# Flat matmul operands, two tiles for the recurrence's values, and the memory's operand made in another stage of a two-layer decoder trunk

## The chip, the cores and the metric

One NeuronCore of one Trainium2 chip runs the whole program. The metric is the device time of one execution in microseconds (us); smaller is better. TensorE (PE) multiplies matrices out of SBUF into PSUM, VectorE (DVE) and ScalarE (ACT) do elementwise work and read PSUM, GpSimd (POOL) does a little elementwise work, and SyncE (SP) issues the DMA transfers. Each engine works through its own instructions in order, and the engines wait for one another by semaphores.

## The reference, cut to what matters

Sequence 256, width 1024, two layers. Each layer runs five sub-layers on the residual stream x:

```python
x = x + 0.5 * swiglu(rms_norm(x, ffn1_norm[l]), ffn1_w_gu[l], ffn1_w_down[l])
z = rms_norm(x, mix_norm[l]) @ w_in[l]
y_a = dilated_attention(q_a, k_a, v_a) @ w_att_branch[l]
o_b = rms_norm(hgrn2_recurrence(q_b, f_b, i_b, lb_all[l]), head_norm) * silu(og_b)
y_b = o_b @ w_hgrn_branch[l]
x = x + (sigmoid(gate_a) * y_a + sigmoid(gate_b) * y_b) @ w_mix_out[l]
x = x + cross_attention(rms_norm(x, xattn_norm[l]), rms_norm(mem, mem_norm[l]), wq, wkv, wo)
x = x + 0.5 * swiglu(rms_norm(x, ffn2_norm[l]), ffn2_w_gu[l], ffn2_w_down[l])
```

The result is a last rms_norm of x. All is float32; the memory `mem` (256 tokens) is an input and the same for both layers.

## The kernel before

The weights are streamed once. A chunk of 16 weight blocks of 128x128 (1 MB) is loaded by SP into `raws`; for each half of a chunk (8 blocks) ACT casts a high part (`whi`, L104) and DVE subtracts it to get a low part (`wlo`, L110). Operands are split in the same way: an `Act` holds for each block of 128 features 256 columns of high and 256 columns of low part side by side, two blocks to a buffer of the pool `big` (23 buffers, named `slot`).

A feature-major product (`fm`, L308 to L323) takes one or two columns of weight blocks. For each block PE runs the high part against the operand's 512 columns (L320) and the low part against its 256 high columns (L321); both add up in PSUM. PSUM is the pool `psum` with four tiles of 1024 columns (`pair`); `bank()` takes a whole such tile and uses half of it. When a product is done, ACT copies one half out (L327), and DVE adds the other at the next tick (L330).

The order of the work beside the products is set by ticks. `Stream.take` calls `tick` once for each half chunk, so once for 8 weight blocks. Each engine's instructions are then in program order (`manual_schedule`). A tick runs deferred work that is due, and then one step of `urgent`, or else one step of a generator in `sides`. While something is urgent, finished products wait with their evacuation.

Four of these pieces bear on the change:

- **The norms.** A sub-layer's operand is x times a gain; the factor of the rms norm is found beside the first products. `Norm.steps` sums squares on PE (L368), takes DVE's mean (L371), POOL's power (L374) and DVE's diagonal (L377), and one tick later PE broadcasts it (L382) and ACT copies it (L384). Eight sub-layers have one, and the memory's statistics have one more (`keep`).
- **The recurrence.** `hgrn` runs twice a layer. At L648 and L650 PE makes the values of the two halves of the sequence, i = 0 and i = 1, in the two halves of one `pair`; ACT squares each half (L652). The tile is read once more by DVE at L661 at a later step.
- **The branches.** After all products from `w_in`, `mixer` multiplies the two branches into the merged operand `mg` (12 blocks for each of 8 columns j) and then multiplies by `w_mix_out`. For each j ACT runs L327 and L275, DVE L330, L866, L868 and L278.
- **The memory's operand.** `mem_operand` loads `mem` (two transfers of 512 KB) and, four steps later, makes the high and low parts of 8 blocks in four steps of two (L285 on ACT, L286 on DVE). It is put in `sides` as the branches begin, so it runs beside them; `xattn` uses it.

```python
both_tiles = pair()
bs = [both_tiles[:, :512], both_tiles[:, 512:]]
```

Of the kernel before, what the change touches and what calls it, by code (L numbers as in the profile page):

```python
# [16 lines left out]
T = 256  # L17
# [110 lines left out]
def build(tc, a, nchunks):  # L128
    nc = tc.nc
    ctx = ExitStack()  # L130
    ent = ctx.enter_context
# [1 line left out]
    raws = ent(tc.tile_pool(name="raws", bufs=3))  # L133
    his = ent(tc.tile_pool(name="his", bufs=5))
    los = ent(tc.tile_pool(name="los", bufs=4))
    big = ent(tc.tile_pool(name="big", bufs=23))
    mid = ent(tc.tile_pool(name="mid", bufs=4))
    tmps = ent(tc.tile_pool(name="tmps", bufs=10))
    tiny = ent(tc.tile_pool(name="tiny", bufs=2))
# [7 lines left out]
    def tmp():  # L147
        return tmps.tile([P, T], F32, name="tmp")

    def pair():  # L150
        return psum.tile([P, 1024], F32, name="pair")

    def bank():
        return pair()[:, :512]

    def join():
        return joins.tile([P, 2 * T], F32, name="join")

    def two(t):
        return t.rearrange("p (i t) -> p i t", i=2)  # L160

    def both(t):
        return t[:, None].to_broadcast([P, 2, T])

    deferred, sides, flags = [], [], set()
# [4 lines left out]
    def defer(n, fn):  # L170
        deferred.append([n, fn])
# [127 lines left out]
    def after(evac):  # L299
        pending.append(evac)  # L300
        if not urgent:
            flush()
# [5 lines left out]
    def fm(items, evac):  # L308

        b = pair().rearrange("p (i h t) -> p i h t", i=2, h=2)
        ks = [item[4] for item in items]
        order = [(k, i) for k in range(max(ks)) for i in range(len(items)) if k < ks[i]]
        if len(set(ks)) > 1:
            order.sort(key=lambda o: o[1])
        for k, i in order:
            name, l, c, act, K = items[i]
            wh, wl = W.take([(name, l, k * P, c)])
            nc.tensor.matmul(b[:, i], wh, two(act.parts(k)), start=k == 0, stop=False)  # L320
            nc.tensor.matmul(b[:, i, 0], wl, act.hi(k), start=False, stop=k == K - 1)  # L321
        n = len(items)
        after(lambda: evac(b[:, :n, 0], b[:, :n, 1]))  # L323

    def add_halves(d, left, right, then, now=False):

        nc.scalar.copy(d, right)  # L327

        def add():
            nc.vector.tensor_tensor(d, left, d, op=OP.add)  # L330
            then()
        if now:
            add()
        else:
            defer(1, add)
# [13 lines left out]
    class Norm:  # L349
# [15 lines left out]
        def steps(self, keep=None):  # L365
            st = bank()
            for i in range(2):
                nc.tensor.matmul(st[:, i:i + 1], self.acc[:, i * P:(i + 1) * P], ones[:, :1],  # L368
                                 start=True, stop=True)
            ms = tiny.tile([P, 2], F32, name="ms")  # L370
            nc.vector.tensor_scalar(ms, st[:, :2], 1.0 / D, EPS, op0=OP.mult, op1=OP.add)  # L371
            pool = tiny if keep is None else consts
            self.r = pool.tile([P, 2], F32, name="rstd" + (keep or ""))
            nc.gpsimd.tensor_tensor(self.r, ms, mhalf[:, :2], op=OP.pow)  # L374
            dg = tmp()
            for i in range(2):
                nc.vector.tensor_scalar(dg[:, i * P:(i + 1) * P], ident, self.r[:, i:i + 1], None, op0=OP.mult)  # L377
            yield
            if keep:
                yield  # L380
            b = bank()
            nc.tensor.matmul(b[:, :T], ones, dg, start=True, stop=True)  # L382
            self.bc = (tiny if keep is None else consts).tile([P, T], F32, name="bc" + (keep or ""))
            nc.scalar.copy(self.bc, b[:, :T])  # L384

    def urgent_norm(n, more=None):
        def run():
            for _ in range(n.wait):
                yield
            yield from n.steps()  # L390
            if more:
                more()
        urgent.append(run())
# [67 lines left out]
    def mm_resid(name, l, act, K, res):  # L461
        n = 2 if K == KD else 1
        for j in range(0, KD, n):
            fm([(name, l, (j + i) * P, act, K) for i in range(n)],
               lambda left, right, j=j: res.take(j, left, right))


    def ffn(pre, l, res, nxt):
        h, n = res.act, res.norm
        urgent_norm(n)  # L470
        act = Act()
        for j in range(KF):
            def evac(left, right, j=j):
                last = j == KF - 1
                t, s = join(), tmp()
                u = t[:, T:]

                def stage1():
                    nc.vector.tensor_tensor(two(t), two(t), both(n.bc), op=OP.mult)  # L479
                    nc.scalar.activation(s, t[:, :T], AF.Silu)  # L480
                    if last:
                        stage2()
                    else:
                        defer(1, stage2)

                def stage2():
                    nc.vector.tensor_tensor(u, s, u, op=OP.mult)
                    act.put(j, u, later=0 if last else 1)
                add_halves(two(t), left, right, stage1, last)
            fm([(pre + "_w_gu", l, c, h, KD) for c in (j * P, FF + j * P)], evac)  # L490
        r = nxt()
        mm_resid(pre + "_w_down", l, act, KF, r)
        return r
# [74 lines left out]
    def mem_operand(l, hm):  # L568
        m = load_mem()
        yield from [None] * 4  # L570
        for j in range(KD):
            hm.put_gain(j, m(j), vec("mem_norm", l, j))
            if j % 2 == 1:
                yield


    def hgrn(l, hh, Q, K, F, ib, sog, out):
# [4 lines left out]
        b = bank()  # L582
# [11 lines left out]
        for li, B in enumerate((1, 2, 4, 8, 16, 32, 64)):  # L594
            W2 = max(2 * B, 32)
            h = W2 // 2
            b = bank()
# [23 lines left out]
            else:  # L621
                for g in range(P // W2):
                    r = slice(W2 * g, W2 * g + B)
                    nc.scalar.copy(lohi(AT)[r, :, W2 * g + B:W2 * g + W2],
                                   b[r, :8 * B].rearrange("p (c u) -> p c u", u=B))
            if B == 16:
                for g in range(4):
                    r = slice(32 * g, 32 * g + 32)
# [3 lines left out]
        b = bank()  # L632
        for h in range(4):
            nc.tensor.matmul(b[:, h * P:(h + 1) * P], lohi(K)[:, 2 * h], lohi(QP)[:, 2 * h + 1],
                             start=True, stop=True)
# [2 lines left out]
        while ("i", l) not in flags:  # L638
            yield True
        ss = tiny.tile([P, 8], F32, name="ss")  # L640
        both_tiles = pair()
        bs = [both_tiles[:, :512], both_tiles[:, 512:]]
        for i in range(2):
            b = bs[i]
            for h in range(4):
# [20 lines left out]
        for i in range(2):  # L666
            b = bank()
# [4 lines left out]
            for h in range(2):  # L672
                k = 4 * hh + 2 * i + h
# [61 lines left out]
    def mixer(l, res, nxt):  # L735
        h, n = res.act, res.norm
# [118 lines left out]
            gate(j)  # L855
        drain()
        mg = Act()
        hm = Act()
        sides.append(mem_operand(l, hm))
        for j in range(KD):  # L860
            def evac(left, right, j=j):
                last = j == KD - 1
# [8 lines left out]
            fm([("w_att_branch", l, j * P, aout, AH), ("w_hgrn_branch", l, j * P, hout, HH)], evac)  # L871
        r = nxt()
        mm_resid("w_mix_out", l, mg, KD, r)
        return r, hm


    def scores(h, q, k):
# [79 lines left out]
    def resid(name, l, scale):  # L957
        return lambda: Resid(lambda j: vec(name, l, j), scale)

    r = resid("ffn1_norm", 0, 0.5)()  # L960
# [18 lines left out]
        yield from lower_bounds()  # L979
    sides.append(setup())  # L980
    for l in range(L):
        r = ffn("ffn1", l, r, resid("mix_norm", l, 0.5))
        r, hm = mixer(l, r, resid("xattn_norm", l, 1.0))
        r = xattn(l, r, hm, resid("ffn2_norm", l, 1.0))
        r = ffn("ffn2", l, r, resid("ffn1_norm", l + 1, 0.5) if l + 1 < L else Last)
    ctx.close()
# [62 lines left out]
```

## Time and profile before

| what | value |
|---|---|
| median of 3 runs | 1673.91 us (1673.47 to 1674.52) |
| the profiled execution's own time | 1671.91 us |
| its span | 1670.1 us |
| PE busy | 1638.0 us, 98% |
| PE weight loads busy | 1417.4 us, 85% |
| DVE busy | 1243.2 us, 74% |
| ACT busy | 924.5 us, 55% |
| mean granted clock of TensorE | 0.995 |

The span is the time from the first to the last instruction of the program; the execution's own time has 1.8 us more around it. Matmuls are pipelined and their ends are modelled, so a busy PE says little: what counts is from one matmul's start to the next one's. A wait is listed as the idle time of an engine before an instruction, with the instruction that ended it.

### The profile page before, as it was taken

The numbers are of one execution on the slowest core, as the hardware profiler recorded it, in microseconds if no ns is written. First come the engines' busy times: TensorE is split into PE (matmuls) and PEld (weight loads), VectorE is DVE, ScalarE is ACT, GpSimd is POOL, SyncE is SP. The second block draws the span as 40 slices with busy tenths as digits, with TensorE's granted clock in tenths as the row PEclk, the third lists the DMA queues.
The fourth block names the chain that finished last, engine by engine and source line by source line (L and its number), as shares of the span: only waits on it lengthen the run. The fifth ranks groups of instructions, "written<-read, shape, count | busy, mean of one in ns | idle before, by whom it ended". The sixth has DMA issues, their size and how long they took to land.

```text
span 1670.1 us, 26491 instructions
## 1 busy us (share of the span) xinstructions
PE 1638.0 (98%) x10818; PEld 1417.4 (85%) x10818; DVE 1243.2 (74%) x1813; ACT 924.5 (55%) x1389; POOL 77.3 (5%) x61
## 2 busy tenths in 40 slices
PE   8999999999998999999999999999999989999998
PEld 7888888888887888888888888888888878888887
DVE  8886696767868868776677767867687688687764
ACT  6665445556665555555456544446565656565542
POOL 2000000111100000000000000010110000000000
PEclk9999999999999999999999999999999999999999
DMA  7555544443444544555455555444444445354552
GB/s 285 186 184 192 185 163 167 152 177 137 166 168 153 184 152 165 189 179 200 177 180 198 184 194 178 168 145 167 152 152 156 172 168 186 126 200 179 184 190 80
DMA packets 41738, 288.94 MB, mean 173 GB/s; under 512 B 4881, under 2 KB 5009, under 8 KB 7441
## 3 DMA queue, kind: packets, MB, share of 16 engines
q1 hardware_dynamic: 41328, 286.73, 47.5%
q8 instruction: 85, 1.39, 0.3%
q10 hardware_dynamic: 288, 0.52, 0.1%
q14 instruction: 37, 0.29, 0.1%
HBM read 286.18 MB, written 1.05 MB: 172 GB/s over the span
## 4 chain that ended last, share of the span: by engine, by line
PE 77%; DVE 11%; issue 8%; ACT 2%; POOL 1%; DMA 1%; SPq 0%; POOLq 0%; ACTq 0%; DVEq 0%
PE pair L320 41%; PE pair L321 21%; DVE wlo L110 4%; PE pair L295 3%; PE pair L297 3%; PE pair L296 3%; PE pair L603 1%; DVE join L330 1%; DVE slot L286 1%; DVE join L866 1%; PE pair L688 1%; PE pair L722 1%; DVE x L407 1%; DMA raw<-w 1%; PE pair L648 0%
## 5 line engine op out<-in xcount | busy, mean ns | idle before, releaser
L320 PE MATMUL pair<-slot,whi 128*128 128x512 f32 x3840 | 1362.0, 399 | 8.2 <-DVE slot L278 7.2
L321 PE MATMUL pair<-slot,wlo 128*128 128x256 f32 x3840 | 1077.0, 280 | 5.6 <-DVE wlo L110 3.9
L320 PEld LDWEIGHTS pair<-slot,whi 128*128 128x128 f32 x3840 | 724.1, 189 | 179.1 <-ACT whi L104 7.8
L321 PEld LDWEIGHTS pair<-slot,wlo 128*128 128x128 f32 x3840 | 727.1, 189 | 9.7 <-DVE wlo L110 5.2
L110 DVE TENSOR_TENSOR wlo<-raw,whi 128x1024 fp32r<-128x1024 f32 x532 | 641.1, 1221 | 40.4 <-ACT whi L104 39.7
L104 ACT CAST whi<-raw 128x1024 fp32r<-128x1024 f32 x532 | 545.6, 1046 | 24.0 <-issue 9.5
L330 DVE TENSOR_TENSOR join<-pair,join 128x512 f32<-128x512 f32 x136 | 93.8, 689 | 108.4 <-ACT join L327 108.3
L327 ACT COPY join<-pair 128x512 f32<-128x512 f32 x136 | 79.4, 585 | 171.7 <-PE pair L321 171.7
L285 ACT ACTIVATE slot<-x,vecs 128x256 fp32r<-128x256 f32 x64 | 30.8, 505 | 141.8 <-DVE x L407 139.3
L295 PE MATMUL pair<-whi,slot 128*128 128x512 f32 x224 | 89.8, 401 | 0.0
L297 PE MATMUL pair<-whi,slot 128*128 128x512 f32 x224 | 87.6, 391 | 0.0
L296 PE MATMUL pair<-wlo,slot 128*128 128x512 f32 x224 | 87.5, 391 | 0.0
L407 DVE SCALAR_TENSOR_TENSOR x<-pair,x 128x256 f32<-128x256 f32 (+1 forms) x80 | 42.5, 531 | 59.4 <-PE pair L321 57.9
L275 ACT CAST slot<-join 128x256 fp32r<-128x256 f32 (+1 forms) x120 | 51.9, 435 | 52.5 <-DVE join L868 30.6
L480 ACT ACTIVATE tmp<-join 128x256 f32<-128x256 f32 x88 | 36.6, 418 | 54.6 <-DVE join L479 54.6
L327 ACT COPY slot<-pair 128x512 f32<-128x512 f32 x48 | 28.0, 583 | 67.8 <-PE pair L321 67.8
L479 DVE TENSOR_TENSOR join<-join,bc 128x512 f32<-128x512 f32 x88 | 60.9, 692 | 3.0
L824 POOL TENSOR_TENSOR join<-join,sinb 128x512 f32<-128x512 f32 x24 | 45.0, 1876 | 378.7 <-ACT join L823 378.7
L330 DVE TENSOR_TENSOR slot<-pair,slot 128x512 f32<-128x512 f32 x48 | 33.1, 689 | 35.6 <-ACT slot L327 35.6
L278 DVE TENSOR_TENSOR slot<-join,slot 128x256 fp32r<-128x256 f32 (+1 forms) x120 | 54.0, 454 | 2.8 <-ACT slot L275 2.8
L286 DVE SCALAR_TENSOR_TENSOR slot<-x,vecs,slot 128x256 fp32r<-128x256 f32 x64 | 31.9, 520 | 27.1 <-ACT slot L285 27.0
L297 PEld LDWEIGHTS pair<-whi,slot 128*128 128x128 f32 x224 | 42.1, 188 | 9.1
(177 smaller groups left out, 1007.5 us busy)
## 6 DMA issues: line engine op xcount, KB each, us to landing
raw<-w SPq DMA_DIRECT2D x267, 1024.0 KB, 4.8
slot<-mem SPq DMA_DIRECT2D x6, 512.0 KB, 6.9
x<-x SPq DMA_DIRECT2D x4, 256.0 KB, 5.7
raw<-w SPq DMA_DIRECT2D x4, 256.0 KB, 7.0
cst<-cst SPq DMA_DIRECT2D x1, 721.0 KB, 11.8
y<-slot ACTq DMA_DIRECT2D x2, 256.0 KB, 2.2
y<-slot SPq DMA_DIRECT2D x2, 256.0 KB, 2.2
posi<-positions SPq DMA_DIRECT2D x1, 128.0 KB, 9.2
```

What stands on the lines that cost most here:

```text
L104: nc.scalar.copy(self.hi[i], r)
L110: nc.vector.tensor_tensor(self.lo[i], r, self.hi[i].bitcast(F32), op=OP.subtract)
L278: nc.vector.tensor_tensor(l, src, h.bitcast(F32), op=OP.subtract)
L295: nc.tensor.matmul(out, ah, wh, start=first, stop=False)
L296: nc.tensor.matmul(out, ah, wl, start=False, stop=False)
L297: nc.tensor.matmul(out, al, wh, start=False, stop=last)
L320: nc.tensor.matmul(b[:, i], wh, two(act.parts(k)), start=k == 0, stop=False)
L321: nc.tensor.matmul(b[:, i, 0], wl, act.hi(k), start=False, stop=k == K - 1)
L327: nc.scalar.copy(d, right)
L330: nc.vector.tensor_tensor(d, left, d, op=OP.add)
L407: nc.vector.scalar_tensor_tensor(x, half, self.scale, x, op0=OP.mult, op1=OP.add)
L479: nc.vector.tensor_tensor(two(t), two(t), both(n.bc), op=OP.mult)
```

## The change

It does five things. The operands of the feature-major products are written as flat runs of 512 columns. The recurrence's values get two tiles in place of the two halves of one. Every norm yields one more tick between its sums and its broadcast, as the memory's did before. The memory's operand is put in `sides` between the two products of the first feed-forward and no longer at the branches. `big` has 27 buffers, and to make room the scratch space for dynamic DMA is set to 1024 bytes.

```diff
-    big = ent(tc.tile_pool(name="big", bufs=23))
+    big = ent(tc.tile_pool(name="big", bufs=27))
...
-        b = pair().rearrange("p (i h t) -> p i h t", i=2, h=2)
+        whole = pair()
+        b = whole.rearrange("p (i h t) -> p i h t", i=2, h=2)
...
-            nc.tensor.matmul(b[:, i], wh, two(act.parts(k)), start=k == 0, stop=False)
-            nc.tensor.matmul(b[:, i, 0], wl, act.hi(k), start=False, stop=k == K - 1)
+            nc.tensor.matmul(whole[:, i * 512:(i + 1) * 512], wh, act.parts(k), start=k == 0, stop=False)
+            nc.tensor.matmul(whole[:, i * 512:i * 512 + T], wl, act.hi(k), start=False, stop=k == K - 1)
...
             yield
-            if keep:
-                yield
+            yield
             b = bank()
...
-    def ffn(pre, l, res, nxt):
+    def ffn(pre, l, res, nxt, beside=None):
...
+        if beside:
+            sides.append(beside())
         r = nxt()
         mm_resid(pre + "_w_down", l, act, KF, r)
...
-        both_tiles = pair()
-        bs = [both_tiles[:, :512], both_tiles[:, 512:]]
+        bs = [bank(), bank()]
...
         mg = Act()
-        hm = Act()
-        sides.append(mem_operand(l, hm))
...
-        r = ffn("ffn1", l, r, resid("mix_norm", l, 0.5))
-        r, hm = mixer(l, r, resid("xattn_norm", l, 1.0))
+        hm = Act()
+        r = ffn("ffn1", l, r, resid("mix_norm", l, 0.5), lambda: mem_operand(l, hm))
+        r = mixer(l, r, resid("xattn_norm", l, 1.0))
...
-    nc = _bacc.Bacc("TRN2", target_bir_lowering=False, num_devices=1)
+    nc = _bacc.Bacc("TRN2", target_bir_lowering=False, num_devices=1, dynamic_dma_scratch_size=1024)
```

The lines of the changed kernel are off by one or two (L320 becomes L321, L330 L331, L648 L649, L866 L865). Three places show what moves.

PE at the first recurrence's values in layer 0, with the semaphores that each instruction waits for; the first two rows are the last weight block of the product before it. Before:

```order
L320 MATMUL pair<-slot,whi 128x512
L321 MATMUL pair<-slot,wlo 128x256
L648 MATMUL pair<-slot 128x128 [waits Activation_49,Pool_49]
L648 MATMUL pair<-slot 128x128 x3
L648 MATMUL pair<-slot 128x128 [waits Activation_49]
L650 MATMUL pair<-slot,tt 128x128
```

And now:

```order
L321 MATMUL pair<-slot,whi 128x512
L322 MATMUL pair<-slot,wlo 128x256
L649 MATMUL pair<-slot 128x128 [waits Activation_49,Pool_49]
L649 MATMUL pair<-slot 128x128 x3
L649 MATMUL pair<-slot 128x128 [waits DVE_49,PE_49]
L651 MATMUL pair<-slot,tt 128x128
```

The fifth values matmul, the first of i = 1, waited for ACT and now waits for whoever had its own tile before. The two rows of the product are the same: a shape has one number for each step of an operand's layout, and it was 128x512 already.

ACT at the norm of the mixer in layer 0, from the end of the feed-forward on (L104 casts a half chunk, so one stands for 8 weight blocks; L384 copies the broadcast; L327 empties a product). Before:

```order
L285 ACTIVATE slot<-x,vecs 128x256
L360 ACTIVATE tmp<-x 128x256
L104 CAST whi<-raw 128x1024 x4
L384 COPY bc<-pair 128x256
L327 COPY join<-pair 128x512 x2
L104 CAST whi<-raw 128x1024
```

And now:

```order
L285 ACTIVATE slot<-x,vecs 128x256
L361 ACTIVATE tmp<-x 128x256
L104 CAST whi<-raw 128x1024 x5
L384 COPY bc<-pair 128x256
L328 COPY join<-pair 128x512 x2
L104 CAST whi<-raw 128x1024
```

The copy of the broadcast, and with it the first two products' evacuation, comes one half chunk later.

DVE at the branches in layer 0, from the third column j on. Before:

```order
L110 TENSOR_TENSOR wlo<-raw,whi 128x1024
L278 TENSOR_TENSOR slot<-join,slot 128x256
L286 SCALAR_TENSOR_TENSOR slot<-slot,vecs 128x256 x2
L110 TENSOR_TENSOR wlo<-raw,whi 128x1024
L330 TENSOR_TENSOR join<-pair,join 128x512
L866 TENSOR_TENSOR join<-join,slot 128x512
L868 TENSOR_TENSOR join<-join 128x256
L286 SCALAR_TENSOR_TENSOR slot<-slot,vecs 128x256 x2
L110 TENSOR_TENSOR wlo<-raw,whi 128x1024
```

And now:

```order
L110 TENSOR_TENSOR wlo<-raw,whi 128x1024
L278 TENSOR_TENSOR slot<-join,slot 128x256
L110 TENSOR_TENSOR wlo<-raw,whi 128x1024
L331 TENSOR_TENSOR join<-pair,join 128x512
L865 TENSOR_TENSOR join<-join,slot 128x512
L867 TENSOR_TENSOR join<-join 128x256
L110 TENSOR_TENSOR wlo<-raw,whi 128x1024
```

All four pairs of L286 are gone from the branches; they stand in the second product of the first feed-forward now, between its L110 and L407. On SP the two transfers of `mem` move in front of the weights of that product, ahead of what they stood behind.

## Rows read from the trace of the kernel before

**Rows 1.** The page: the chain of work that ended last, by engine.
```profile
PE 77%; DVE 11%; issue 8%; ACT 2%; POOL 1%; DMA 1%; SPq 0%; POOLq 0%; ACTq 0%; DVEq 0%
```

**Rows 2.** PE's waits: line, awaited line, us in total, times, longest.
```profile
PE pair L320 <- DVE slot L278: 7.2, 2, 4.3
PE pair L321 <- DVE wlo L110: 3.9, 2, 2.0
PE pair L648 <- ACT tt L652: 2.7, 4, 0.7
PE pair L382 <- DVE tmp L377: 2.4, 6, 0.7
```

**Rows 3.** Timeline of PE, branches of layer 0: start, duration, instruction, [idle before].
```profile
505.22 0.40 PE L320 MATMUL pair<-slot,whi 128*128 128x512 f32 x1
507.56 0.39 PE L321 MATMUL pair<-slot,wlo 128*128 128x256 f32 x1 [1.93 <-DVE wlo L110]
...
521.38 0.28 PE L321 MATMUL pair<-slot,wlo 128*128 128x256 f32 x1
524.59 0.47 PE L320 MATMUL pair<-slot,whi 128*128 128x512 f32 x1 [2.93 <-DVE slot L278]
```

**Rows 4.** Timeline of DVE, the same stretch.
```profile
495.73 0.88 DVE L286 SCALAR_TENSOR_TENSOR slot<-slot,vecs 128x256 fp32r<-128x256 f32 x2 [0.36 <-ACT slot L285]
496.54 1.22 DVE L110 TENSOR_TENSOR wlo<-raw,whi 128x1024 fp32r<-128x1024 f32 x1
...
500.42 0.89 DVE L286 SCALAR_TENSOR_TENSOR slot<-slot,vecs 128x256 fp32r<-128x256 f32 x2 [0.88 <-ACT slot L285]
...
505.48 0.88 DVE L286 SCALAR_TENSOR_TENSOR slot<-slot,vecs 128x256 fp32r<-128x256 f32 x2 [0.89 <-ACT slot L285]
```

**Rows 5.** Stretches: length; PE, PEld, DVE, ACT, POOL busy; granted clock; DMA.
```profile
140.00:205.00 65.00, 65.00 (x379) 56.89 (x378) 42.71 (x60) 31.96 (x43) 0.44 (x1) 1.00 0.50 181
...
508.00:511.00 3.00, 3.00 (x11) 2.58 (x10) 2.97 (x5) 1.01 (x2) 0.00 (x0) 0.50 0.71 273
525.00:528.00 3.00, 3.00 (x12) 2.53 (x11) 1.41 (x3) 0.00 (x0) 0.00 (x0) 0.51 0.32 109
```

**Rows 6.** Timeline of PE, branches of layer 1.
```profile
1331.19 0.39 PE L321 MATMUL pair<-slot,wlo 128*128 128x256 f32 x1 [1.97 <-DVE wlo L110]
1331.41 0.39 PE L320 MATMUL pair<-slot,whi 128*128 128x512 f32 x1
...
1343.66 0.28 PE L321 MATMUL pair<-slot,wlo 128*128 128x256 f32 x1
1348.23 0.77 PE L320 MATMUL pair<-slot,whi 128*128 128x512 f32 x1 [4.29 <-DVE slot L278]
```

**Rows 7.** Timeline of PE at cross-attention's norm in layer 1.
```profile
1375.96 0.27 PE L321 MATMUL pair<-slot,wlo 128*128 128x256 f32 x1
1376.07 0.40 PE L320 MATMUL pair<-slot,whi 128*128 128x512 f32 x1
1376.30 0.28 PE L321 MATMUL pair<-slot,wlo 128*128 128x256 f32 x1
1377.30 0.67 PE L382 MATMUL pair<-tmp,cst 128*128 128x256 f32 x2 [0.71 <-DVE tmp L377]
```

**Rows 8.** Timeline of PE, then DVE, at the second attention of layer 0.
```profile
387.74 1.46 PE L688 MATMUL pair<-slot 128*128 128x256 f32 x6
...
387.94 0.56 DVE L693 SCALAR_TENSOR_TENSOR slot<-pair,cst 128x384 f32<-128x384 f32 x1 [0.27 <-PE pair L684]
```

**Rows 9.** Timeline of ACT, then DVE: a product of layer 0 is emptied.
```profile
384.50 0.59 ACT L327 COPY slot<-pair 128x512 f32<-128x512 f32 x1 [2.41 <-PE pair L321]
...
385.11 0.69 DVE L330 TENSOR_TENSOR slot<-pair,slot 128x512 f32<-128x512 f32 x1 [1.33 <-ACT slot L327]
```

**Rows 10.** Timeline of PE: two token-major matmuls of 512 flat columns.
```profile
300.03 0.39 PE L295 MATMUL pair<-whi,slot 128*128 128x512 f32 x1
300.26 0.39 PE L296 MATMUL pair<-wlo,slot 128*128 128x512 f32 x1
```

More of the change, by code (lines that the diff above doesn't have):

```diff
@@ L873, in mixer @@
         mm_resid("w_mix_out", l, mg, KD, r)
-        return r, hm
+        return r
     def scores(h, q, k):
```

## The prediction, made before the changed kernel ran

> **What bounds the kernel now.** I read the page first. PE is busy 98% of the span (the table) and makes up 77% of the last chain; DVE holds 11% of it [rows 1]. So the weights' products set the time, and a change can gain in two ways: PE does a product faster, or it stops waiting. The view of PE's waits comes next. Four of its rows touch lines of the change [rows 2]: L320 waits for DVE's L278 twice, 7.2 us together, L321 for DVE's L110 twice, 3.9 us, L648 for ACT's L652 four times, 2.7 us, and L382 for DVE's L377 six times, 2.4 us. Together 16.2 us of 1670.
>
> The first two are the largest, and the timeline places them: in each layer both lie at the branches [rows 3, 6]. From start to start PE loses in layer 0 2.34 - 0.23 = 2.1 us at 505.22 and 3.21 - 0.11 = 3.1 us at 521.38, in layer 1 again 2.1 us before 1331.19 and 4.57 - 0.11 = 4.5 us at 1343.66 (0.23 and 0.11 us are what L320 and L321 take from start to start when nothing waits [rows 7]). DVE's timeline shows who is late [rows 4]: the memory's operand (L286) sits between L110 and the branches' own work, and three times out of four DVE even stands still before it, 0.36, 0.88 and 0.89 us, until ACT has made the high part.
>
> The stall costs more than its length where the clock falls. After the idle 1.93 us in layer 0 the granted clock is 0.50 from 508 to 511, and after the idle 2.93 us it is 0.51 from 525 to 528 [rows 5]: that is the 1.2 GHz level, at which 3 us do the work of 1.5. After the idle 1.97 us in layer 1 the next L320 takes 0.39 us as always [rows 6], so there it did not fall.
>
> **The change part by part.** The profiled execution took 1671.9 us; the median of the runs shown is 2.0 us above it. The sum is made against the first.
>
> *Flat operands:* nothing. The order shows the product's shape as 128x512 before and now, so the layout was already merged into one run. The trace agrees: a flat token-major matmul starts 0.23 us after the one before it [rows 10], and L320 takes 0.23 us to the next start as well [rows 7].
>
> *The memory's operand leaves the branches.* DVE works without a pause there but for its waits, so what bounds PE is DVE's chain. It gets shorter by the idle 0.36 + 0.88 + 0.89 = 2.13 us and by four pairs of 0.81 us (495.73 to 496.54) [rows 4], 5.4 us in each layer, 10.7 us in both. Not all waiting goes. In layer 0 PE would come to the last wait earlier by the 2.1 us of the first stall and some 1.8 us for the half clock (3 us at 0.50 lose 1.5, the edges a little more), while DVE comes 5.4 us earlier: a wait of 3.1 + 3.9 - 5.4 = 1.6 us stays. In layer 1 it is 4.5 + 2.1 - 5.4 = 1.2 us. What is late there is the merged operand's last columns: copy L327, L330, L866, L868, ACT's L275, L278. The half clock after the second stall, 1.5 us a layer, goes or stays with this wait; 1.93 us brought it once and 1.97 us did not, so I count half, 1.5 us over both layers. The part gains **12.2 us**; the bounds are 10.7 - 4.3 = 6.4 us, if DVE's idle 2.13 us reappear at other waits for ACT, and 10.7 + 3.0 + 1.3 = 15 us, if clock and the rest of the wait go almost wholly.
>
> *Where it goes to.* In the first feed-forward's second product DVE is busy 42.7 of 65 us and ACT 32.0 [rows 5], and PE is never idle. The eight L286 and L285 add 3.2 and 3.6 us to that stage, and weights are cast two and three half chunks ahead, each half chunk being 2.8 us of PE's time. I cost it at nothing; without that cover it would cost what it does now. The two transfers go past the weights' queue on SP before that product. The four added buffers of the pool are the ones this operand occupies, so the transfers need not wait for a reader. The scratch size has no instruction; the memory operand has the same eight blocks as before.
>
> *One more tick at the norms.* PE's L382 comes 8 blocks, 2.8 us, later, and the longest wait for the diagonal is 0.7 us [rows 2], so all six waits go: 2.4 us, and at each the cut of 0.17 us (L321 takes 0.28 us alone, 0.11 in a stream; 1376.30 to 1377.30 is 1.00 us in place of 0.11 [rows 7]). Gain **3.4 us**. What it delays is the evacuation of the first two products, which now both wait for the broadcast. The fourth product then needs the first one's tile; two ticks, 5.6 us, lie between, and copy and add took 1.30 us (384.50 to 385.80) [rows 9]. I take nothing, and at most 0.9 us (1.00 - 0.11) for each of eight norms, the nearest row's loss of a late norm.
>
> *Two tiles for the values.* L648 for i = 1 waits four times up to 0.7 us, 2.7 us in all, for ACT's square of i = 0 [rows 2], since both are in one tile; with a cut of 0.15 us each, an estimate after the one above, the gain is **3.3 us**. The price: of four PSUM tiles the recurrence now holds two until L661. At the second attention of each layer one more is being written by the product, so its two score tiles, which now lie apart, have one place between them: L688 must wait until DVE has read what L684 made. DVE's read ends at 387.94 + 0.56 = 388.50, and L688 started at 387.74 [rows 8]: 0.8 us, twice, a loss of **1.6 us**; behind it on PE stands the next product. The bounds are 0 and 3 us (DVE's L110 in front of that read).
>
> The sum is 12.2 + 3.4 + 3.3 - 1.6 = 17.3 us: 1654.6 us for such an execution, and with the 2.0 us **1656.6 us** as a median.
>
> **The rivals.** *DVE stays the bound at the branches.* For it speaks that each column goes from DVE to ACT's L275 and back, so DVE could stand still without L285 too; against it that its waits of that stretch name L285 [rows 4]. Then the branches give 6.4 us with no clock gain: 1662.4 us.
>
> *The norms pay for the later evacuation.* 3.4 us turn into a loss of up to 8 x 0.9 = 7.2 us when the fourth product waits for a tile; two such norms would already eat half the gain. Taken at half, 3.6 us lost in place of none: 1660.2 us; in full 1663.8 us.
>
> *The work moved is not hidden.* L407, which empties a tile of the second product, stands behind L286 on DVE. If PE waits there for all 5.4 us a layer, the time is 1667.3 us. Against it: 22 us of idle DVE in that stage [rows 5].
>
> *PSUM runs out, and it is slower.* While the recurrence holds two tiles (371 to 399 us in layer 0), all products, levels and attention pieces take turns on two places. Each needs the tile of the last but one, whose emptying takes 1.3 us when ACT and DVE are free [rows 9] against 2.8 us for 8 blocks of PE. If copies queue behind other work for over 2.8 us, PE waits at each. To end slower by 0.2% the four recurrences must cost 17.3 + 3.3 = 20.6 us, 5.2 us each, with some five tiles 1 us late. It decides from a lag of about 3.8 us on; that gives 1677 us and more. Against it: no row of PE's waits names a product's copy or add before. The Trainium skill (Trainium Kernel Development and Optimization, Best Practices) says that consistent bubbles can mean that SBUF or PSUM ran out. The trace of before shows no such bubbles, with three places to turn on.
>
> *The flat operand counts after all.* If the layout with two steps cost L320 anything, the rows allow 0.01 us, the last digit in which L320 and the flat matmul agree [rows 7, 10]; 3840 of them would be 38 us, and the time 1618 us. The order's equal shapes speak against it. The Trainium skill (PSUM — Partial Sum Buffer, Specifications (TRN2)) says that a non-contiguous access pattern slows matmuls significantly, which would make this rival of the edit if its layout were one.
>
> **How the numbers follow.** Forecast 68%; DVE stays the bound 11%; norms 8%; moved work not hidden 6%; PSUM 5%; flat operands 2%. The forecast's own range is 1650 (15 us at the branches, the attention's wait halved, some 2 us of scatter between executions) to 1660. Up to 1664 it takes in the first two rivals; outside stay moved work, PSUM, flat operands and tails, under 20%. About 0.2%, 3.3 us, is what a measurement can tell from no change: same is 1670.6 to 1677.3. Only half-hidden mixtures and a mild PSUM case fall there, 5%; slower 4%; faster 91%.
>
> **What would show it.** In the changed profile no row of PE waiting for L652 or L377; at the branches no wait for L110, and one for L278 of 1 to 2 us a layer; a new wait of L689 for the scores' first read, twice near 0.8 us; PE without idle time in the first feed-forward's second product. L321 still 0.23 us from start to start. Wrong would be: many short waits of PE for the copy or add of a product between the values and L662, or waits of 3 us and more left at the output projection.

## The result, and the profile after

The changed kernel takes 1649.89 us (median of 4 runs, 1648.78 to 1651.13) against 1673.69 us of the kernel before (4 runs, 1672.21 to 1674.52): a ratio of 0.9861, 95% interval 0.9848 to 0.9873. The forecast was 1656.6 us. The sign was right, but 23.8 us were gained where 17.1 us were forecast, and the time lies at the lower edge of the forecast's own range of 1650 to 1660 us: the median is 0.1 us below it, and the ratio applied to the earlier 1673.91 us gives 1650.6 us, just inside. The profiled execution of the change took 1648.78 us, its span is 1647.0 us.

The page of the changed kernel, first the busy times, then the chain that ended last:

```profile
PE 1625.8 (99%) x10818; PEld 1415.1 (86%) x10818; DVE 1242.5 (75%) x1813; ACT 924.6 (56%) x1389; POOL 77.0 (5%) x61
...
PE 85%; DVE 9%; ACT 2%; issue 2%; POOL 0%; DMA 0%; SPq 0%; POOLq 0%; ACTq 0%; DVEq 0%
```

PE's share of the chain rises from 77% to 85%, and "issue" falls from 8% to 2% [rows 1]. The number of matmuls is unchanged, so the gain is waits and pace, not work. PE's waits in the changed kernel (L320 before is L321 now, L321 is L322, L368 is L369):

```profile
PE pair L321 <- DVE slot L278: 3.2, 2, 1.9
PE pair L222 <- ACT warm L219: 2.3, 1, 2.3
PE pair L369 <- DVE tmp L363: 2.0, 1, 2.0
...
PE pair L689 <- DVE slot L694: 1.3, 2, 0.7
```

Of the four rows of before [rows 2] three are gone: the waits for L110 at the branches, for ACT's square of the values, and all six of the norms' broadcast. The wait for L278 fell from 7.2 to 3.2 us. L689, the scores' wait that was forecast twice near 0.8 us, is there twice with up to 0.7 us. L369 sums the memory's squares; it waited 0.7 us once before (as L368) and waits 2.0 us now, which was not foreseen.

A view by stages shows where the gain fell. It is worked out from the two traces: the time from the first product matmul of a stage to the first of the next, in us.

| stage | layer 0 before | after | layer 1 before | after |
|---|---|---|---|---|
| ffn1, first product | 130.50 | 132.11 | 123.07 | 123.01 |
| ffn1, second product | 61.01 | 61.01 | 61.01 | 61.01 |
| `w_in`, recurrence, attention | 281.28 | 280.27 | 282.07 | 280.78 |
| branches | 37.82 | 33.28 | 36.36 | 33.92 |
| `w_mix_out` | 26.93 | 24.38 | 28.11 | 24.07 |
| cross-attention without `wo` | 82.15 | 80.75 | 81.64 | 80.82 |
| `wo` | 22.61 | 22.61 | 22.61 | 22.61 |
| ffn2, first product | 125.81 | 123.13 | 125.82 | 123.13 |
| ffn2, second product to the end of the stage | 62.18 | 61.01 | 72.40 | 72.24 |

Branches and `w_mix_out` gain 13.6 us, `w_in` 2.3, cross-attention 2.2, and ffn2 6.7, while ffn1's first product loses 1.6 in layer 0: with 0.1 lost at the start and in roundings that is the 23.1 us between the spans.

**The branches.** PE's timeline in the changed kernel, at `w_mix_out` in layer 0 and layer 1:

```profile
517.55 0.28 PE L322 MATMUL pair<-slot,wlo 128*128 128x256 f32 x1
519.78 0.47 PE L321 MATMUL pair<-slot,whi 128*128 128x512 f32 x1 [1.95 <-DVE slot L278]
...
1329.75 0.47 PE L321 MATMUL pair<-slot,whi 128*128 128x512 f32 x1 [1.23 <-DVE slot L278]
```

One wait a layer is left, 1.95 and 1.23 us, where 1.6 and 1.2 were forecast. The stretches right behind them (length; PE, PEld, DVE, ACT, POOL busy; granted clock; DMA):

```profile
519.00:522.00 3.00, 2.22 (x13) 2.00 (x14) 2.32 (x4) 0.60 (x1) 0.00 (x0) 1.00 0.19 27
...
1330.00:1333.00 3.00, 3.00 (x18) 2.58 (x18) 2.12 (x3) 0.12 (x1) 0.00 (x0) 1.00 0.36 96
```

The granted clock stays at 1.00 behind both, the 2.4 GHz level. Before, it was 0.50 and 0.51 behind layer 0's two waits [rows 5]; in layer 1 it was 1.00 behind the first and 0.50 behind the 4.29 us:

```profile
1332.00:1335.00 3.00, 3.00 (x19) 2.63 (x18) 2.93 (x5) 0.65 (x1) 0.00 (x0) 1.00 0.89 311
1348.00:1351.00 3.00, 2.77 (x9) 2.41 (x10) 1.22 (x2) 0.05 (x1) 0.00 (x0) 0.50 0.16 33
```

**Where the work went.** In ffn1's second product, where the memory's operand is made now, PE is busy through (the changed kernel, layer 0 and 1, same columns), and the stage takes the same 61.01 us as before:

```profile
140.00:200.00 60.00, 60.00 (x349) 52.91 (x348) 41.85 (x62) 30.69 (x46) 0.00 (x0) 1.00 0.57 207
950.00:1009.00 59.00, 59.00 (x342) 52.00 (x341) 41.42 (x61) 30.80 (x46) 0.00 (x0) 1.00 0.57 205
```

**A gain that no term names.** ffn2 gains 6.7 us, more than its two norm waits. PE's timeline before, around the norm's broadcast in ffn2 of layer 0:

```profile
657.84 0.28 PE L321 MATMUL pair<-slot,wlo 128*128 128x256 f32 x1
658.45 0.67 PE L382 MATMUL pair<-tmp,cst 128*128 128x256 f32 x2 [0.33 <-DVE tmp L377]
...
659.31 0.40 PE L320 MATMUL pair<-slot,whi 128*128 128x512 f32 x1
...
660.37 0.40 PE L320 MATMUL pair<-slot,whi 128*128 128x512 f32 x1
```

and after:

```profile
652.90 0.28 PE L322 MATMUL pair<-slot,wlo 128*128 128x256 f32 x1
653.01 0.59 PE L382 MATMUL pair<-tmp,cst 128*128 128x256 f32 x2
...
654.14 0.39 PE L321 MATMUL pair<-slot,whi 128*128 128x512 f32 x1
...
655.18 0.39 PE L321 MATMUL pair<-slot,whi 128*128 128x512 f32 x1
```

Before, three blocks of the product take 660.37 - 659.31 = 1.06 us, after 655.18 - 654.14 = 1.04 us, with nothing waited for in either. The pace lasts: a stretch of 100 us in that product holds 567 matmuls before and 579 after, at a granted clock of 1.00 in both.

```profile
680.00:780.00 100.00, 100.00 (x567) 86.79 (x566) 75.78 (x106) 58.12 (x89) 0.00 (x0) 1.00 0.51 182
```

```profile
680.00:780.00 100.00, 100.00 (x579) 88.17 (x578) 75.84 (x105) 57.61 (x86) 0.00 (x0) 1.00 0.53 192
```

The 176 blocks of the second product say it without an edge: 62.18 / 176 = 0.3533 us a block before, 61.01 / 176 = 0.3466 after. I call these the slower and the faster step. Which part of the change brings the faster one is the question the first experiments had to answer.

### The profile page after: what moved, and what is told of

It is laid out like the page before. It is cut to its first block, busy times and chain, and to the rows that moved or that the text cites. A ratio compares the mean times of both kernels' runs of the same rounds, so it can differ in the third digit from the quotient of the medians.

```text
span 1647.0 us, 26504 instructions
## 1 busy us (share of the span) xinstructions
PE 1625.8 (99%) x10818; PEld 1415.1 (86%) x10818; DVE 1242.5 (75%) x1813; ACT 924.6 (56%) x1389; POOL 77.0 (5%) x61
## 4 chain that ended last, share of the span: by engine, by line
PE 85%; DVE 9%; ACT 2%; issue 2%; POOL 0%; DMA 0%; SPq 0%; POOLq 0%; ACTq 0%; DVEq 0%
PE pair L321 46%; PE pair L322 24%; PE pair L295 3%; DVE wlo L110 3%; PE pair L297 3%; PE pair L296 3%; DVE join L331 1%; PE pair L605 1%; DVE join L865 1%; PE pair L689 1%; PE pair L723 1%; DVE slot L278 0%; PE pair L293 0%; PE pair L292 0%; PE pair L291 0%
## 5 line engine op out<-in xcount | busy, mean ns | idle before, releaser
L321 PE MATMUL pair<-slot,whi 128*128 128x512 f32 x3840 | 1352.7, 396 | 4.7 <-DVE slot L278 3.2
L322 PE MATMUL pair<-slot,wlo 128*128 128x256 f32 x3840 | 1075.5, 280 | 1.6 <-DVE wlo L77 1.6
L321 PEld LDWEIGHTS pair<-slot,whi 128*128 128x128 f32 x3840 | 719.4, 187 | 168.6 <-ACT whi L104 3.8
L322 PEld LDWEIGHTS pair<-slot,wlo 128*128 128x128 f32 x3840 | 725.2, 189 | 4.3 <-DVE wlo L77 3.4
L110 DVE TENSOR_TENSOR wlo<-raw,whi 128x1024 fp32r<-128x1024 f32 x532 | 641.3, 1220 | 44.1 <-ACT whi L104 39.5
L104 ACT CAST whi<-raw 128x1024 fp32r<-128x1024 f32 x532 | 546.5, 1047 | 34.1 <-issue 14.4
L331 DVE TENSOR_TENSOR join<-pair,join 128x512 f32<-128x512 f32 x136 | 93.7, 689 | 96.1 <-ACT join L328 95.9
L328 ACT COPY join<-pair 128x512 f32<-128x512 f32 x136 | 79.0, 587 | 148.9 <-PE pair L322 148.9
L407 DVE SCALAR_TENSOR_TENSOR x<-pair,x 128x256 f32<-128x256 f32 (+1 forms) x80 | 42.4, 530 | 49.0 <-PE pair L322 47.5
L328 ACT COPY slot<-pair 128x512 f32<-128x512 f32 x48 | 28.0, 583 | 69.0 <-PE pair L322 69.0
L331 DVE TENSOR_TENSOR slot<-pair,slot 128x512 f32<-128x512 f32 x48 | 33.0, 688 | 35.7 <-ACT slot L328 35.7
L278 DVE TENSOR_TENSOR slot<-join,slot 128x256 fp32r<-128x256 f32 (+1 forms) x120 | 54.0, 454 | 2.8 <-ACT slot L275 2.8
L286 DVE SCALAR_TENSOR_TENSOR slot<-x,vecs,slot 128x256 fp32r<-128x256 f32 x64 | 32.1, 523 | 27.0 <-ACT slot L285 27.0
```

The lines of the kernel that those rows point to most:

```text
L104: nc.scalar.copy(self.hi[i], r)
L110: nc.vector.tensor_tensor(self.lo[i], r, self.hi[i].bitcast(F32), op=OP.subtract)
L278: nc.vector.tensor_tensor(l, src, h.bitcast(F32), op=OP.subtract)
L321: nc.tensor.matmul(whole[:, i * 512:(i + 1) * 512], wh, act.parts(k), start=k == 0, stop=False)
L322: nc.tensor.matmul(whole[:, i * 512:i * 512 + T], wl, act.hi(k), start=False, stop=k == K - 1)
```

## The experiments

### One part at a time

Each of the first four makes one part of the change alone in the kernel before. The kernel before took 1673.74 us beside them (21 runs).

```diff
...
-            nc.tensor.matmul(b[:, i], wh, two(act.parts(k)), start=k == 0, stop=False)
...
+            nc.tensor.matmul(whole[:, i * 512:(i + 1) * 512], wh, act.parts(k), start=k == 0, stop=False)
...
```

> The kernel before with the flat operands alone. The order shows the same instructions, so the first theory (the gain of 23 us is the waits that went) expects 0 us, within 1.5 us, and the second feed-forward's products at the same slow step as before (567 matmuls of PE from 680 to 780 us). The rival, that the layout counts, expects 3840 times up to 0.01 us, so up to 38 us less. A third reading, that the slow step of that stage is a chance of one execution, expects about 579 matmuls there in some repetition, this one perhaps.

Measured: 1672.52 us, ratio 0.9995 (0.9987 to 1.0004). The flat operands do nothing that these runs can tell from none. The slower step stays in ffn2 as well (125.81 and 62.19 us in layer 0), so it comes back in another run and is no accident of one.

```diff
-            if keep:
-                yield
+            yield
```

> The kernel before with the one more tick at the norms alone. First theory: the six waits for the diagonal go (3.8 us from start to start), the memory's sums wait 1.3 us longer, 2.5 us less in all, and the second feed-forward keeps its slow step of 353 ns a block. The rival: a norm that lets PE wait leaves the products behind it in the slower step, and without the wait they run at 347 ns a block; then another 5 us go, 7.5 us less in all, and 680 to 780 us hold about 579 matmuls and not 567.

Measured: 1665.99 us, ratio 0.996 (0.9948 to 0.9973), so 7.7 us. All waits of L382 are gone; ffn2's products take 123.13 and 61.01 us, as in the full change, and the same stretch of 100 us holds 579 matmuls:

```profile
680.00:780.00 100.00, 100.00 (x579) 88.20 (x578) 77.38 (x107) 59.98 (x91) 0.00 (x0) 1.00 0.51 184
```

Of the four parts it is the only one that brings the faster step there. The unforeseen wait belongs to the tick as well; PE's wait in this kernel:

```profile
PE pair L368 <- DVE tmp L362: 2.0, 1, 2.0
```

```diff
-        both_tiles = pair()
-        bs = [both_tiles[:, :512], both_tiles[:, 512:]]
+        bs = [bank(), bank()]
```

> The kernel before with two tiles for the recurrence's values alone. First theory: four waits of L648 go (3.8 us from start to start) and two waits of 0.8 us at the second attention come, 2.1 us less. The rival that the faster step comes with this part expects 5 us more than that, 7 us less.

Measured: 1671.03 us, ratio 0.9982 (0.9973 to 0.9991). The wait for ACT's square is gone and the forecast one of the scores is there (L687 is the changed kernel's L689); ffn2 keeps the slower step.

```profile
PE pair L687 <- DVE slot L692: 1.3, 2, 0.7
```

For the memory's operand, the hunks of the change on `ffn`, `mixer`, the main loop, the pool and the scratch size alone:

```diff
-        sides.append(mem_operand(l, hm))
...
+        if beside:
+            sides.append(beside())
```

> The kernel before with the memory's operand in the first feed-forward alone (27 buffers and the small scratch with it). First theory: the branches lose 7.0 us and the output projection 6.6 us in both layers together, 13.6 us less; waits of 1.2 to 2 us stay at the projection; the first feed-forward's second product keeps 61.0 us. The rival that the faster step of the second feed-forward comes with this part (the buffers lie elsewhere) expects 5 us more, 18.6 us less.

Measured: 1659.06 us, ratio 0.9916 (0.9902 to 0.993), so 14.7 us. PE's waits in this kernel have no row for L110 at the branches, and for L278:

```profile
PE pair L320 <- DVE slot L278: 2.4, 2, 1.2
```

The clock at `w_mix_out` of layer 0 stays whole in it too:

```profile
517.00:525.00 8.00, 6.78 (x39) 5.69 (x38) 6.16 (x10) 4.68 (x9) 0.00 (x0) 1.00 0.36 130
```

The four parts come to 1.2 (within its interval of none) + 7.7 + 2.7 + 14.7 = 26.3 us, the whole change to 23.8 us; they add up within what these runs resolve (by the intervals each of the four gains is known to some 1.4 to 2.3 us).

### What is left, and a better version

Three edits of the changed kernel aim at three of its remaining waits, and one run has them all. The kernel before took 1670.73 us beside them (7 runs, on another chip), 3 us less than in the comparisons so far, so ratios are compared.

```diff
-        bs = [bank(), bank()]
+        both_tiles = pair()
+        bs = [both_tiles[:, :512], both_tiles[:, 512:]]
...
+        for i in range(2):
             sq = mid.tile([P, 512], F32, name="tt")
-            nc.scalar.activation(sq, b, AF.Square)
+            nc.scalar.activation(sq, bs[i], AF.Square)
```

> The changed kernel with one tile of two halves for the recurrence's values again, but with the eight products of both halves issued ahead of ACT's squares and DVE's sums, so that L648 waits for no reader although the tile is one. Theory: the second tile cost the second attention its place (PE's wait of L689 for L694, 1.3 us in two waits, with the cut of 0.15 us each some 1.6 us) and nothing else; that wait goes, no wait of L648 comes back, time 1649.9 - 1.6 = 1648.3 us. Rival: the place is not what L689 waits for, since two places are held in any case while three tiles turn; the wait of L689 stays, time 1649.9 us. A second rival: ACT's squares, later by four matmuls, make something else late, waits of L661's readers on PE, 1651 us or more.

Measured: 1648.01 us, ratio 0.9857 (0.9842 to 0.9871), which the median can't tell from the change's 0.9861. The trace can: no wait of L689 and none for the square of the values is left, and the two `w_in` stages take 0.96 and 0.95 us less. (Two waits of 0.3 us that the kernel before had at L670 for L675, and the change had not, are back.) So the order of PE's and ACT's instructions does what the second tile did, and the second tile's price was the place it took.

```diff
-                    mg.put(j, m, later=0 if last else 1)
+                    mg.put(j, m, later=0 if j >= KD - 2 else 1)
```

> The changed kernel with the low part (L278) of the merged operand's column 6 made at once, not a tick later, as that of column 7 is. Theory: the last wait at the output projection (L321 for L278, 1.95 us in layer 0 and 1.23 us in layer 1) is DVE's order, column 6's L278 standing behind column 7's L110; without it some 1.2 us a layer go, time 1649.9 - 2.4 = 1647.5 us, the wait for L278 below 1 us in each layer. Rival: column 7's own chain (copy, L330, L866, L868, ACT's L275, L278) sets the end; the same wait stays under the same name, and column 6's low part only goes ahead of it, 1649.9 to 1650.9 us.

Measured: 1646.74 us, ratio 0.985 (0.9835 to 0.9864); `w_mix_out` falls to 22.62 us in both layers, by 1.76 and 1.45 us, and the wait for L278 is gone. The interval overlaps the change's, so it is the trace that shows the gain. Not all of the 1.76 us is the edit's: in the change's execution layer 0's branches ran the faster step (33.28 us), here the slower one (33.92), and taken together the two stages gain 1.1 and 1.5 us; the spans differ by 2.6 us. DVE's timeline shows why the wait went, first in the changed kernel:

```profile
517.74 0.42 DVE L278 TENSOR_TENSOR slot<-join,slot 128x256 fp32r<-128x256 f32 x1 [0.47 <-ACT slot L275]
518.08 1.22 DVE L110 TENSOR_TENSOR wlo<-raw,whi 128x1024 fp32r<-128x1024 f32 x1
519.22 0.42 DVE L278 TENSOR_TENSOR slot<-join,slot 128x256 fp32r<-128x256 f32 x1
```

then in this one:

```profile
515.28 0.43 DVE L278 TENSOR_TENSOR slot<-join,slot 128x256 fp32r<-128x256 f32 x1 [0.47 <-ACT slot L275]
...
518.11 0.42 DVE L278 TENSOR_TENSOR slot<-join,slot 128x256 fp32r<-128x256 f32 x1 [0.47 <-ACT slot L275]
518.46 1.22 DVE L110 TENSOR_TENSOR wlo<-raw,whi 128x1024 fp32r<-128x1024 f32 x1
```

Column 6's low part (the second L278 of the first view, the first of the other) stood behind the low part of a half chunk of weights (L110, 1.22 us) for which PE waits in neither kernel.

```diff
             yield
+        yield
         yield
         yield from n.steps(keep="mem")
```

> The changed kernel with one more step of the side work between the memory's last square and the matmuls that sum it (L369). Theory: PE's one wait of 2.0 us for DVE's L363 near 97 us is a matter of one tick only, it goes, and with its cut of 0.17 us the time is 1649.9 - 2.2 = 1647.7 us. Rival: the side work moves on as a whole and the next one of it (tables, lower bounds) waits in its place, or the changed phase brings the slower step of the product stream into one more stage (about 2.7 us for a feed-forward's first product); 1649.9 to 1652 us.

Measured: 1648.13 us, ratio 0.9863 (0.9844 to 0.9882): the median shows nothing. The wait of L369 is gone and ffn1's first product takes 130.23 us in place of 132.11; the span is 2.0 us shorter. A wait of 0.3 us of the memory's broadcast (L382) is new, so a little of the rival came with it. In the main the theory holds in the trace; that the time gains is not shown by this run alone.

> The changed kernel with the three edits of the runs beside it together: one tile for the values with its products ahead of the squares, column 6's low part at once, the memory's sums one step later. Theory: the waits that go are apart in time, so the gains add, 1649.9 - 1.6 - 2.4 - 2.2 = 1643.7 us. Rival: some stage falls into the slower step of the product stream (353 ns a block in place of 347), which gives back 1.2 to 2.7 us for each product of a feed-forward; 1645 to 1649 us, with the stage's duration showing it at full clock.

Measured: 1642.05 us, ratio 0.9823 (0.9809 to 0.9838), an interval wholly below the change's 0.9848 to 0.9873. This version beats both kernels: 28.7 us less than before, where the change gained 23.8 in its own comparison. Its span is 1640.2 us, 6.8 less than the change's; 6.2 had been expected. ffn1's first product (129.91), `w_in` (279.06 and 279.74) and `w_mix_out` (22.62 twice) show the three edits apart, and the feed-forwards keep the faster step.

### What sets the step

```diff
+    def nudge():
+        b = bank()
+        nc.tensor.matmul(b[:, :T], warm[:, :P], warm, start=True, stop=True)
+        yield
...
+        if pre == "ffn2":
+            sides.append(nudge())
```

> The kernel before with one added float32 matmul of 128x256 (zeros from the warm-up, result unread) in each second feed-forward, issued one tick behind the norm's broadcast, when its operands have long been there. Its two traces so far show the step of the product stream change only at the broadcast L382: where L382 came at once the next blocks took 347 ns, where it had waited 0.39 us for DVE they went on at 353 ns. Theory: what changes the step is a float32 matmul in the stream without a wait ahead of it; the added one does that, so the second feed-forward's first product falls from 125.8 to about 123.9 us in each layer and the second product of layer 0 from 62.2 to 61.0; about 5 us less, 1668.7 us where the kernel before takes 1673.7. Rival: the step belongs to the later evacuation or to the wait being gone, not to the matmul; the slower step stays and the added work shows, 126.2 us for the product, 1674.5 us in all.

Measured: 1668.22 us against 1672.96 (10 runs), ratio 0.9968 (0.9956 to 0.998): more work, and 4.7 us less. ffn2 takes 124.10 us twice and 61.01 us. The step turns at the added matmul (L463); PE's timeline in this kernel:

```profile
661.37 0.40 PE L320 MATMUL pair<-slot,whi 128*128 128x512 f32 x1
...
662.43 0.40 PE L320 MATMUL pair<-slot,whi 128*128 128x512 f32 x1
...
662.78 0.59 PE L463 MATMUL pair<-warm 128*128 128x256 f32 x2
...
663.56 0.40 PE L320 MATMUL pair<-slot,whi 128*128 128x512 f32 x1
...
663.91 0.39 PE L320 MATMUL pair<-slot,whi 128*128 128x512 f32 x1
...
664.25 0.40 PE L320 MATMUL pair<-slot,whi 128*128 128x512 f32 x1
```

1.06 us for three blocks ahead of it, 0.69 us for two behind it (0.71 at the slower step). The norm's waits are all still there (L382 2.3 us in six; 0.33 us ahead of ffn2's broadcast in the kernel before, not the 0.39 named above), so the faster step doesn't need them gone.

```diff
-            self.wait = 2
+            self.wait = 3
```

> The kernel before with three ticks in place of two ahead of the norms' sums, so that the sums, the broadcast and the evacuation behind it all come one tick later, as the evacuation does in the change, but the broadcast stands one tick behind the sums as before and waits for DVE's diagonal. Theory: the wait ahead of L382 keeps the slower step, so the second feed-forward's products stay at 125.8 and 62.2 us, the waits of L382 for L377 stay near 2.4 us in all, and the time stays within 1 us of the kernel before. Rival: the later place of the norm, or the later evacuation, brings the faster step; 123.1 and 61.0 us there and about 5 us less in all.

Measured: 1664.82 us, ratio 0.9951 (0.9938 to 0.9963): my theory missed, and the run could not decide what it was made for. Of the waits of L382 only two at `w_in` are left, 0.4 us together, which I had ruled out; so they depend on where in DVE's work the norm falls, not on the ticks between sums and broadcast alone. The run gains 8.1 us, as much as the change's tick alone (7.7), and keeps the memory's wait at 0.7 us. In layer 1 the step of ffn2 turns at the broadcast, which came at once; in layer 0 it turns at another place, behind the sums (L368), ahead of the broadcast:

```profile
656.91 0.50 PE L368 MATMUL pair<-cst,tmp 128*128 128x1 f32 x4
...
658.06 0.39 PE L320 MATMUL pair<-slot,whi 128*128 128x512 f32 x1
...
659.79 0.39 PE L320 MATMUL pair<-slot,whi 128*128 128x512 f32 x1
```

Five blocks take 659.79 - 658.06 = 1.73 us (1.77 at the slower step), and the two products take 123.08 and 61.01 us. In ffn2 of the kernel before and of the change the same four matmuls turn nothing.

The traces of all 13 kernels say more when the blocks ahead of and behind every such place are timed (six blocks on either side, from the second behind it on). The broadcast or the added matmul, both float32 of 128x256, came 86 times without a wait; the blocks behind ran the faster step every time, 55 times after the slower one. The broadcast came 35 times after a wait of 0.17 to 0.71 us; behind it were 13 times the faster and 22 times the slower step. Behind the sums it can be either: in ffn1 of layer 1 of the change they turn the faster step into the slower one. So the theory of the run before this one holds for matmuls of that size wherever the traces can check it: what the tick gave ffn2 is a broadcast that comes at once. Why it acts so inside PE is not shown.

The same added matmul at the branches' first blocks of the best version:

```diff
         drain()
+        sides.append(nudge())
         mg = Act()
```

> The kernel of the run f4_all_three with the same added float32 matmul at the first blocks of the branches in each layer. There the branches and the output projection behind them, 160 blocks, run in the slower step (33.92 and 22.62 us). Theory: the added matmul brings the faster step, 6.6 ns a block from there, about 1.0 us a layer, less some 0.3 us that it takes itself; branches and projection 33.55 and 22.19 us in place of 33.92 and 22.62, the time 1.4 us below f4_all_three. Rival: the faster step comes only behind a real norm in a feed-forward; 34.2 and 22.62 us, the time 0.6 us above it.

Measured: 1644.08 us, ratio 0.9826 (0.9812 to 0.9839): no difference to 0.9823. The branches take 33.48 us twice and `w_mix_out` 22.47 and 22.45, for 0.6 us a layer in place of 0.7. The faster step holds through the branches, but it is lost again in `w_mix_out`, in layer 0 at a block that takes 0.53 us, with no foreign matmul there and the granted clock at 1.00 on both sides:

```profile
528.43 0.39 PE L321 MATMUL pair<-slot,whi 128*128 128x512 f32 x1
...
529.47 0.39 PE L321 MATMUL pair<-slot,whi 128*128 128x512 f32 x1
529.78 0.39 PE L322 MATMUL pair<-slot,wlo 128*128 128x256 f32 x1
530.00 0.39 PE L321 MATMUL pair<-slot,whi 128*128 128x512 f32 x1
...
531.06 0.40 PE L321 MATMUL pair<-slot,whi 128*128 128x512 f32 x1
```

Three blocks take 1.04 us ahead of it and 1.06 us behind it, so a short delay alone can turn the step. The span is 2.0 us longer. ffn1's products in layer 0, which lie ahead of the edit and hold the same instructions in the same order, take 130.60 and 62.19 us in place of 129.91 and 61.01: there this execution kept the slower step behind the memory's broadcast, which waited 0.26 us here; in the best version it waited 0.30 us and the faster step followed. That is not the edit's doing by any path I can name; whether it is chance or the other chip on which this run was timed is not shown.

## Why the prediction was right, and where it was off

By the spans 23.1 us were gained against the sum's 17.3, 5.8 us more; and the median after is 1.1 us above its profiled execution where 2.0 had been added, 0.9 us. That makes the 6.7 us between forecast and result. The 5.8 us are 4.6 at the norms' tick and 1.4 at the memory's operand, less 0.2 elsewhere.

- **Flat operands, 0:** right, shown by the run of that part (ratio 0.9995). The rival that gave 38 us is out. The Trainium skill's rule that a non-contiguous access pattern slows matmuls (PSUM — Partial Sum Buffer, Specifications (TRN2)) has no case here, since the order shows one run of 128x512 before and after.
- **Memory's operand, 12.2 us:** the mechanism was right, with the waits that were to stay (1.95 and 1.23 us for 1.6 and 1.2). I had counted half of the clock's 3.0 us as gained; the clock fell at neither wait, so all of it was, and the stretch gave 13.6 us, inside the bounds of 6.4 to 15 (the run of that part alone gained 14.7 us in all). That the clock stayed whole behind 1.95 us, when it had fallen behind 1.93 us before, no run explains; that share of the gain may be luck. The rival in which DVE stays the bound is out.
- **Where it goes to, 0:** right; 61.01 us before and after in both layers.
- **The norms' tick, 3.4 us:** the term that failed, by its size. The waits went as forecast, for 3.9 us from start to start; by the stages it is cross-attention 2.2 us, some 0.9 at `w_in` (0.42 and 0.49 in the run of the tick alone) and 0.5 at each ffn2 (658.45 - 657.84 = 0.61 us in place of 0.11), 4.1 us. But the faster step gives 2 x (2.69 - 0.50) + 1.17 = 5.5 us more, and L369 takes 1.6 us back in ffn1's first product. The term was 8.0 us, 4.6 more than its 3.4; the run of the tick alone gained 7.7 us. I had taken the step from start to start of two rows (0.23 and 0.11 us) as a constant of the product; it has two values, and the two digits of those rows hide it. That the tick would change the step, by letting the broadcast come without a wait, stood in no term and no rival.
- **Later evacuation, 0:** right; no row of PE's waits names a product's copy (L328) or add (L331).
- **Two tiles for the values, 3.3 - 1.6 = 1.7 us:** right in both signs; `w_in` gained 2.3 us, 0.9 of them by the norm, which leaves 1.4. The rival in which PSUM runs out is out: the only new wait for a tile is that of L689, 1.3 us in two. The consistent bubbles of which the Trainium skill speaks (Trainium Kernel Development and Optimization, Best Practices) don't appear.

Left open: why the stream has two steps at all, and what decides between them where it was interrupted by a wait, a short delay or the sums.

## What to carry to other kernels

Compare stage by stage before explaining a total: a gain in a stage that the edit hardly touches is a mechanism you have not named yet. A stall of PE at a stage's end is often one small instruction standing behind a big one that nobody waits for; look at the other engine's order there before adding buffers. And where a shared tile makes a writer wait for a reader, issuing the writes ahead of the reads can do what a second tile does, without its place.

## What the runs showed of the hardware

- A stream of 128x512 and 128x256 matmuls with a weight load each ran in two steps that hold for hundreds of blocks at a granted clock of 1.00: 0.3466 and 0.3533 us a block (176 blocks in 61.01 and 62.18 us). Behind a float32 matmul of 128x256 that came into the stream without a wait it was the faster one, 86 times of 86; behind one that had waited, either. `wo` ran the slower one in every kernel of this study (22.61 us for 64 blocks).
- The granted clock does not follow the length of an idle stretch alone: behind 1.93 us it was 0.50 [rows 5], the 1.2 GHz level; behind 1.97 us [rows 6] and 1.95 us it stayed at 1.00, the 2.4 GHz level.
